# PSUM operands, a gate tile moved ahead of the attention, a shared score bank and chunks begun early, in a two-block fp32 transformer kernel

## The chip, the cores and the metric

The kernel runs on one core of a Trainium2 chip. The metric is the device time of one execution, in microseconds. The kernel before took 1399.2 us (median of 3 runs, 1398.55 to 1399.31).

## The reference

Two blocks work on one sequence of 512 tokens of width 1024, in fp32. The change touches the first block and the places where the blocks and their halves join:

```
mod = silu(c) @ ada_w + ada_b             # 6 rows of 1024: sh1 sc1 ga1 sh2 sc2 ga2
h = rmsnorm(x) * (1 + sc1) + sh1
glu, qkv, gates = split(h @ w_in)         # conv input, attention input, 2 x 1024 gate columns
u = silu(layernorm(causal_conv_31_taps(val * sigmoid(gate))))
z = q k^T / 8                             # stick-breaking attention, 8 heads of 64
a[t,s] = sigmoid(z[t,s]) * prod over s < j < t of sigmoid(-z[t,j])      # s < t
y = (sigmoid(g_conv) * (u @ w_conv_out) + sigmoid(g_att) * (a v @ w_att_out)) @ w_o
x = x + ga1 * rmsnorm(y)                  # boundary 1
x = x + ga2 * rmsnorm(swiglu(h2))         # h2 from rmsnorm(x), sc2, sh2; boundary 2
x = x + w_out(retention, latent attention); x = x + conv_ffn(rmsnorm(x))   # boundary 3 between
```

The second block and a last norm follow; their sources are unchanged.

## The kernel before, in words

Every fp32 product is three fp32r products (`mm3`, L202 to L205): high part by high part, low by high and high by low. A weight slab of 128x1024 is loaded by SP into `w_st`, ACT makes its high part `w_hi` (L185), and DVE or POOL the low part `w_lo` (L208). A weight tile is 8 x 3 = 24 products of 512 columns into one PSUM bank. There are 8 banks in three rings: `psT` with 2 (transposes, attention-by-value, modulation chunks), `psP` with 4 (function `pp()`: weight tiles and scores) and `psC` with 2 (convolution accumulators, later weight tiles too). The calls are written out in program order, and a scheduler orders each engine's instructions from a timing model of its own, so the queues below differ in places from the order of the source. Each engine then works its queue in order.

The stick-breaking stage (108 to 270 us): `stick_head` is a generator of three steps. In the first, for each of four query blocks `i` of 128, it takes a bank, writes (i+1)x128 score columns by three matmuls, and ACT writes sigmoid(-z) to `kp` and sigmoid(z) to `sp` (SBUF). DVE scans `kp` backwards into a running product (L739), and POOL (heads 0 to 5) or DVE multiplies `sp` by it (L743). The second step transposes the four blocks, the third multiplies by the values. `pipeline` runs the third step of head t-2, the second of t-1 and the first of t, and then `stick_between(t)`: weight tiles by the table `STICK_FILL` (q and k tiles of the next head pair, `g` gate tiles, `c` tiles of w_conv_out), some taps of the convolution, and modulation chunks by the table `AD`. The convolution's four channel blocks have 31 taps each: for blocks 0 to 2 one DVE operation a tap (L543, accumulator in PSUM), for block 3 a tap on ACT and an add on POOL (L547). Its sums `cacc` are then transposed on PE (L229) for the layer norm.

A modulation chunk (`ada_acc`) is 256 columns of `ada_w`, loaded as two halves `ad` of 512 KB. In mode "pe", 16 matmuls sum it over the rows (L376), in mode "dve" 8 DVE operations (L386, L388); then `ada_cols` or `ga_row` sums over the partitions by a matmul with `ones`, at once. In the merge (270 to 342 us), chunks run in mode "dve" behind each of four steps `p`. Steps 2 and 3 have two gate tiles and a w_conv_out slab each, every step has a w_att_out slab (24 products) and the gating on DVE and POOL.

At a boundary, `update` takes the two 512-column banks of a row tile: two squares on ACT give the norm, DVE multiplies by it and by the gate row into `y` (SBUF, L332), and `x + y` is done by DVE for the first half and by POOL for the second (L335). `boundary` then squares the 1024 new columns (`norm_of`) and scales them into `xn`, which PE transposes. Boundary 3 has no gate row: DVE adds straight from PSUM (L326).

Of the kernel before, what the change touches and what calls it, by code (L numbers as in the profile page):

```python
# [8 lines left out]
F32 = mybir.dt.float32  # L9
# [3 lines left out]
AF = mybir.ActivationFunctionType  # L13
# [6 lines left out]
KB = 8  # L20
# [76 lines left out]
def build(tc, nc, a):  # L97
# [145 lines left out]
    def sumsq(src, jp):  # L243
        ss = sm.tile([128, 1], F32, tag="ss", name="ss")
        n = src.shape[1]
        w = 256 if n <= 256 else 1024
        junk = jp.tile([128, w], BF16, tag=f"junk{w}", name="junk", bufs=1)
        nc.scalar.activation(out=junk[:, :n], in_=src, func=AF.Square, accum_out=ss)
        return ss
# [70 lines left out]
        return hh[:, k, :], hl[:, k, :]  # L320

    def update(banks, tt, x_in, x_out, grow, bp):
        if grow is None:
            for hf in range(2):
                cs = slice(512 * hf, 512 * hf + 512)
                nc.vector.tensor_tensor(out=x_out[:, cs], in0=banks[tt, hf], in1=x_in[:, cs], op=ALU.add)  # L326
            return
# [396 lines left out]
    def stick_head(h):  # L724
        p, b = divmod(h, 2)
        qs, ks, kl = qk[p]
        blocks = []
        for i in range(NT):
            n = (i + 1) * 128
            qb = slice(i * 128, n)  # L730
            z = pp()
            nc.tensor.matmul(out=z[:, :n], lhsT=qs[b][:, qb], rhs=ks[b][:, :n], start=True, stop=False)
            nc.tensor.matmul(out=z[:, :n], lhsT=qs[b][:, qb], rhs=kl[b][:, :n], start=False, stop=False)
            nc.tensor.matmul(out=z[:, qb], lhsT=identr, rhs=strict, start=False, stop=True)
            sp = apool.tile([128, n], F32, tag=f"sp{i}", name="sp")
# [3 lines left out]
            nc.vector.tensor_tensor_scan(  # L739
                out=kp[:, :n][:, ::-1], data0=kp[:, :n][:, ::-1], data1=zero.broadcast_to([128, n]),  # L740
                initial=1.0, op0=ALU.mult, op1=ALU.add,
            )
            (nc.gpsimd if h < 6 else nc.vector).tensor_tensor(  # L743
                out=sp[:, 0:n - 1], in0=sp[:, 0:n - 1], in1=kp[:, 1:n], op=ALU.mult
            )
            blocks.append(sp)
# [725 lines left out]
```

## Time and profile before

| | before |
|---|---|
| median of 3 runs | 1399.2 us (1398.55 to 1399.31) |
| profiled execution | 1396.24 us, span 1394.5 us |
| PE busy | 1351.0 us (97%), 6666 instructions |
| DVE, ACT, POOL busy | 777.8 (56%), 579.7 (42%), 333.1 us (24%) |
| DMA | 152.18 MB, mean 109 GB/s |
| mean granted TensorE clock | 0.992 |

The chain of work that ended last is 82% PE, 7% DVE, 4% ACT. Times are microseconds from the start of the profiled execution's span unless marked ns. A view by stretch gives each engine's busy time within a piece of the span, and PEclk the share of full speed that TensorE was granted there. In a row such as `ps_p<-hh,w_hi` the output stands left of the arrow; a bracket at the end is idle time just before the instruction and what ended it.

### The profile page before, as it was taken

The numbers are of one execution on the slowest core, as the hardware profiler recorded it, in microseconds if no ns is written. First come the engines' busy times: TensorE is split into PE (matmuls) and PEld (weight loads), VectorE is DVE, ScalarE is ACT, GpSimd is POOL, SyncE is SP. The second block draws the span as 40 slices with busy tenths as digits, with TensorE's granted clock in tenths as the row PEclk, the third lists the DMA queues.
The fourth block names the chain that finished last, engine by engine and source line by source line (L and its number), as shares of the span: only waits on it lengthen the run. The fifth ranks groups of instructions, "written<-read, shape, count | busy, mean of one in ns | idle before, by whom it ended". The sixth has DMA issues, their size and how long they took to land.

```text
span 1394.5 us, 17375 instructions
## 1 busy us (share of the span) xinstructions
PE 1351.0 (97%) x6666; PEld 1124.3 (81%) x6666; DVE 777.8 (56%) x1236; ACT 579.7 (42%) x953; POOL 333.1 (24%) x336
## 2 busy tenths in 40 slices
PE   8997999999989999999999999989999999999998
PEld 7786787888788888888887789777888888888886
DVE  5699878386357333323334655787257555554334
ACT  4557555332344222222224427777246433333323
POOL 2389665411150000000003434567020000000000
PEclk9998999999999999999999999999999999999999
DMA  9432133565125334433322332001323323323231
GB/s 339 143 97 67 58 119 107 184 225 183 64 68 174 121 112 130 126 101 91 104 92 82 128 102 87 24 25 46 121 76 122 105 91 100 97 93 104 91 99 68
DMA packets 44691, 152.18 MB, mean 109 GB/s; under 512 B 4913, under 2 KB 7473, under 8 KB 44609
## 3 DMA queue, kind: packets, MB, share of 16 engines
q1 hardware_dynamic: 43008, 146.03, 32.0%
q0 software_dynamic: 1312, 4.77, 1.0%
q8 instruction: 52, 0.85, 0.3%
q10 hardware_dynamic: 288, 0.27, 0.1%
q14 instruction: 31, 0.25, 0.1%
HBM read 146.86 MB, written 4.19 MB: 108 GB/s over the span
## 4 chain that ended last, share of the span: by engine, by line
PE 82%; DVE 7%; ACT 4%; issue 2%; POOL 2%; DMA 2%; SPq 0%; POOLq 0%; ACTq 0%; DVEq 0%
PE ps_p L203 16%; PE ps_p L204 16%; PE ps_p L205 16%; PE ps_c L203 7%; PE ps_c L204 7%; PE ps_c L205 7%; PE ps_t L203 2%; PE ps_t L204 2%; PE ps_t L205 2%; PE ps_t L229 2%; DVE w_lo L208 1%; DVE kp L739 1%; PE ps_t L699 1%; ACT w_hi L185 1%; DMA xs<-in_x 1%
## 5 line engine op out<-in xcount | busy, mean ns | idle before, releaser
L185 ACT CAST w_hi<-w_st 128x1024 fp32r<-128x1024 f32 (+2 forms) x217 | 225.3, 1040 | 386.6 <-PE ps_p L204 142.2
L208 DVE TENSOR_TENSOR w_lo<-w_st,w_hi 128x1024 fp32r<-128x1024 f32 (+2 forms) x179 | 221.6, 1240 | 239.8 <-ACT w_hi L185 238.4
L203 PE MATMUL ps_p<-hh,w_hi 128*128 128x512 f32 (+1 forms) x740 | 276.0, 380 | 4.2 <-ACT hh L264 3.2
L205 PE MATMUL ps_p<-hh,w_lo 128*128 128x512 f32 (+1 forms) x740 | 278.2, 377 | 1.4 <-DVE w_lo L208 1.4
L204 PE MATMUL ps_p<-hl,w_hi 128*128 128x512 f32 (+1 forms) x740 | 279.3, 379 | 0.2 <-POOL hl L208 0.2
L240 POOL TENSOR_TENSOR r<-q,mhalf 128x1 f32<-128x1 f32 x36 | 21.0, 584 | 768.5 <-DVE q L236 717.3
L203 PEld LDWEIGHTS ps_p<-hh,w_hi 128*128 128x128 f32 x740 | 139.4, 190 | 30.3 <-ACT hh L264 3.6
L205 PEld LDWEIGHTS ps_p<-hh,w_lo 128*128 128x128 f32 x740 | 140.8, 190 | 27.1 <-DVE w_lo L208 2.5
L204 PEld LDWEIGHTS ps_p<-hl,w_hi 128*128 128x128 f32 x740 | 140.9, 190 | 25.2 <-issue 0.8
L203 PE MATMUL ps_c<-hh,w_hi 128*128 128x512 f32 (+1 forms) x354 | 129.9, 367 | 3.2 <-ACT hh L264 2.0
L204 PE MATMUL ps_c<-hl,w_hi 128*128 128x512 f32 (+1 forms) x354 | 130.7, 370 | 0.6 <-POOL hl L208 0.6
L205 PE MATMUL ps_c<-hh,w_lo 128*128 128x512 f32 (+1 forms) x354 | 128.7, 364 | 0.0
L208 POOL TENSOR_TENSOR w_lo<-w_st,w_hi 128x1024 fp32r<-128x1024 f32 (+1 forms) x38 | 93.3, 2461 | 58.9 <-ACT w_hi L185 49.3
L208 DVE TENSOR_TENSOR gl<-gf,gh 128x512 fp32r<-128x512 f32 x44 | 30.4, 690 | 105.6 <-ACT gh L919 105.5
L919 ACT CAST gh<-gf 128x512 fp32r<-128x512 f32 x44 | 27.4, 622 | 133.4 <-PE ps_p L204 124.1
L203 PEld LDWEIGHTS ps_c<-hh,w_hi 128*128 128x128 f32 x354 | 67.3, 190 | 14.9 <-ACT hh L264 2.5
L204 PEld LDWEIGHTS ps_c<-hl,w_hi 128*128 128x128 f32 x354 | 67.2, 190 | 11.5 <-POOL hl L208 0.8
L205 PEld LDWEIGHTS ps_c<-hh,w_lo 128*128 128x128 f32 x354 | 67.3, 190 | 10.1
L205 PE MATMUL ps_p<-w_hi,gl 128*128 128x512 f32 x176 | 68.5, 389 | 0.0
L204 PE MATMUL ps_p<-w_lo,gh 128*128 128x512 f32 x176 | 68.5, 389 | 0.0
L203 PE MATMUL ps_p<-w_hi,gh 128*128 128x512 f32 x176 | 68.5, 389 | 0.0
L543 DVE SCALAR_TENSOR_TENSOR ps_c<-upad,vec,ps_c 128x512 f32<-128x512 f32 x87 | 60.6, 746 | 0.8
(430 smaller groups left out, 2579.0 us busy)
## 6 DMA issues: line engine op xcount, KB each, us to landing
ad<-in_ada SPq DMA_DIRECT2D x48, 512.0 KB, 4.1
w_st<-in_w_fin SPq DMA_DIRECT2D x44, 512.0 KB, 3.7
w_st<-in_w_up SPq DMA_DIRECT2D x44, 512.0 KB, 3.5
w_st<-in_w_win SPq DMA_DIRECT2D x22, 512.0 KB, 3.6
w_st<-in_w_fout SPq DMA_DIRECT2D x22, 512.0 KB, 3.6
w_st<-in_w_down SPq DMA_DIRECT2D x22, 512.0 KB, 3.5
w_st<-in_w_gate SPq DMA_DIRECT2D x16, 512.0 KB, 4.3
w_st<-in_w_wo SPq DMA_DIRECT2D x16, 512.0 KB, 3.7
```

Source lines behind the costliest of these rows:

```text
L185: nc.scalar.copy(w_hi[:, :n], w_st[:, :n])
L203: nc.tensor.matmul(out=out, lhsT=lh, rhs=rh, start=start, stop=False)
L204: nc.tensor.matmul(out=out, lhsT=lh, rhs=rl, start=False, stop=False)
L205: nc.tensor.matmul(out=out, lhsT=ll, rhs=rh, start=False, stop=stop)
L208: (eng or nc.vector).tensor_tensor(out=out, in0=src, in1=hi.bitcast(F32), op=ALU.subtract)
L229: nc.tensor.transpose(out=ps[:r, j * 128:(j + 1) * 128], in_=s, identity=ident)
L240: nc.gpsimd.tensor_tensor(out=r, in0=q, in1=mhalf[:, 0:1], op=ALU.pow)
L543: nc.vector.scalar_tensor_tensor(out=out, in0=src, scalar=w, in1=acc, op0=ALU.mult, op1=ALU.add)
L699: nc.tensor.matmul(out=ps[:, kb * 128:S], lhsT=vt(kb, h), rhs=a_slice(at[j], kb, 0, n), start=first, stop=kb == NT - 1 and j == 0,)
L739: nc.vector.tensor_tensor_scan(out=kp[:, :n][:, ::-1], data0=kp[:, :n][:, ::-1], data1=zero.broadcast_to([128, n]), initial=1.0, op0=ALU.m ...
L919: nc.scalar.copy(gh, gf[:, k, :])
```

## The change

Four things are rewritten.

In `stick_head`, blocks 0 and 2 (128 and 384 columns) share a bank, so a head takes three banks; `sp` is computed first, sigmoid(-z) is written over z in the bank, one ACT operation serves both blocks, and the scan reads the bank and writes `kp`. Gate tile 8 comes before head 0, and the tiles of `STICK_FILL` move up.

In `update`, `y` is written back into its bank, both adds are DVE's from PSUM, and each half is squared right after its add; `boundary` takes the norm from the two sums, at all three boundaries.

Chunk 5 of the second modulation goes from slot 8 of the stick stage (mode "pe") to step 0 of the merge (mode "dve"). `ada_cols` and `ga_row` begin a chunk and return the part with the `ones` matmul as a function, which the merge calls behind the step's products. The row chunks of `ga_row` are spread over steps 1 to 3, and three `ad` buffers are used in place of two.

```diff
-STICK_FILL = _fill("q1 k1|g8|q2 k2|g9|q3 k3|g10 g11|g12 g13|g14 g15|g0 g1 c0|g2 g3 c1")
+STICK_FILL = _fill("q1 k1|g9|q2 k2|g10|q3 k3|g11 g12|g13 g14|g15 g0|g1 c0|g2 g3 c1")
...
-ORDER += [("win", 8), ("win", 12)]
+ORDER += [("win", 8), ("win", 12), ("gate", 8)]
...
     def update(banks, tt, x_in, x_out, grow, bp):
-        if grow is None:
...
-        r = rstd(sumsq(banks[tt, 0], bp), sumsq(banks[tt, 1], bp), eps1k)
+        if grow is not None:
+            r = rstd(sumsq(banks[tt, 0], bp), sumsq(banks[tt, 1], bp), eps1k)
+        ss = []
         for hf in range(2):
             cs = slice(512 * hf, 512 * hf + 512)
-            y = bp.tile([128, 512], F32, tag="y", name="y", bufs=2)
...
-            (nc.vector if hf == 0 else nc.gpsimd).tensor_tensor(
-                out=x_out[:, cs], in0=x_in[:, cs], in1=y, op=ALU.add
-            )
+            y = banks[tt, hf]
+            if grow is not None:
+                nc.vector.scalar_tensor_tensor(out=y, in0=y, scalar=r, in1=grow[:, cs], op0=ALU.mult, op1=ALU.mult)
+            nc.vector.tensor_tensor(out=x_out[:, cs], in0=y, in1=x_in[:, cs], op=ALU.add)
+            ss.append(sumsq(x_out[:, cs], bp))
+        return ss
...
-            norm_of(xo, bp, xn)
+            nc.vector.tensor_scalar(out=xn, in0=xo, scalar1=rstd(ss[0], ss[1], eps1k), scalar2=None, op0=ALU.mult)
...
     def ada_cols(i, kb, g_name, ap_):
         acc, ps = ada_acc(8 * i + kb, ap_)
+        return lambda: ada_cols_end(i, kb, g_name, acc, ps)
...
-        for i in range(NT):
-            n = (i + 1) * 128
-            qb = slice(i * 128, n)
+        for grp in ((0, 2), (1,), (3,)):
             z = pp()
...
+            for i in grp:
+                n = (i + 1) * 128
+                qb = slice(i * 128, n)
+                zi = z[:, c0:c0 + n]
...
-            nc.scalar.activation(out=kp[:, :n], in_=z[:, :n], func=AF.Sigmoid, scale=-0.125)
-            nc.scalar.activation(out=sp, in_=z[:, :n], func=AF.Sigmoid, scale=0.125)
-            nc.vector.tensor_tensor_scan(
-                out=kp[:, :n][:, ::-1], data0=kp[:, :n][:, ::-1], data1=zero.broadcast_to([128, n]),
...
+            nc.scalar.activation(out=sp, in_=z[:, :c0], func=AF.Sigmoid, scale=0.125)
+            nc.scalar.activation(out=z[:, :c0], in_=z[:, :c0], func=AF.Sigmoid, scale=-0.125)
+            for i, cs in parts:
+                nc.vector.tensor_tensor_scan(
+                    out=kp[:, cs][:, ::-1], data0=z[:, cs][:, ::-1], data1=zero.broadcast_to([128, 128 * i + 128]),
...
-    AD = (3, 4, 5, 6, 7, 8, 20, 21)
+    AD = (3, 4, 5, 6, 7, 20, 20, 21)
...
+    att_gate(8)
     pipeline([stick_head(h) for h in range(NH)], (2, 1, 0), stick_between)
...
-    ADA.pool, ADA.tag, ADA.bufs, ADA.mode = mtmp, "ad", 2, "dve"
+    ADA.pool, ADA.tag, ADA.bufs, ADA.mode = mtmp, "ad", 3, "dve"
...
     for p in range(4):
+        accs = [accp, mtmp]
+        ends = [ada_cols(1, kb, "pre_ffn_g", accs.pop(0)) for kb in range(KB) if AD[kb] == 20 + p]
+        ends += [ga_row(0, grow1, accs.pop(0), q, mtmp) for q in ((), (0,), (1, 2), (3,))[p]]
...
-        for kb in range(KB):
-            if AD[kb] == 20 + p:
-                ada_cols(1, kb, "pre_ffn_g", accp)
-        for q in ((0,), (1, 2), (3,), ())[p]:
-            ga_row(0, grow1, accp, q, mtmp)
+        for end in ends:
+            end()
```

What moves is seen in the order of the queues. First SP's queue, ahead of the stick stage, before; `win` slabs are q and k tiles, the first two being q0 and k0:

```order
L184 DMA w_st<-in_w_v 128x1024 x2
L184 DMA w_st<-in_w_win 128x1024 x4
L184 DMA w_st<-in_w_gate 128x1024
L184 DMA w_st<-in_w_win 128x1024 x2
L184 DMA w_st<-in_w_gate 128x1024
L184 DMA w_st<-in_w_win 128x1024 x2
L361 DMA ad<-in_ada 128x1024 x2
```

The same place on SP now:

```order
L184 DMA w_st<-in_w_v 128x1024 x2
L184 DMA w_st<-in_w_win 128x1024 x2
L184 DMA w_st<-in_w_gate 128x1024
L184 DMA w_st<-in_w_win 128x1024 x2
L184 DMA w_st<-in_w_gate 128x1024
L184 DMA w_st<-in_w_win 128x1024 x2
L184 DMA w_st<-in_w_gate 128x1024
L184 DMA w_st<-in_w_win 128x1024 x2
L358 DMA ad<-in_ada 128x1024 x2
```

The slab of gate tile 8 is asked for ahead of q1 and k1, and each later gate slab one place sooner.

Second, DVE's queue around the first head, before; `kp<-kp,zero` is a scan (shown by the name of its form), `ps_c` and `cacc` are taps:

```order
L543 SCALAR_TENSOR_TENSOR cacc<-upad,vec,ps_c 128x512
L208 TENSOR_TENSOR kz_918<-ps_p,mv_997 64x512
L739 SCALAR_TENSOR_TENSOR kp<-kp,zero 128x128
L543 SCALAR_TENSOR_TENSOR cacc<-upad,vec,ps_c 128x512
L739 SCALAR_TENSOR_TENSOR kp<-kp,zero 128x256
L543 SCALAR_TENSOR_TENSOR ps_c<-upad,vec,ps_c 128x512
L739 SCALAR_TENSOR_TENSOR kp<-kp,zero 128x384
L543 SCALAR_TENSOR_TENSOR ps_c<-upad,vec,ps_c 128x512 x2
L739 SCALAR_TENSOR_TENSOR kp<-kp,zero 128x512
L543 SCALAR_TENSOR_TENSOR ps_c<-upad,vec,ps_c 128x512 x6
```

DVE's queue around the first head now:

```order
L546 SCALAR_TENSOR_TENSOR cacc<-upad,vec,ps_c 128x512
L208 TENSOR_TENSOR kz_918<-ps_p,mv_997 64x512
L546 SCALAR_TENSOR_TENSOR cacc<-upad,vec,ps_c 128x512
L546 SCALAR_TENSOR_TENSOR ps_c<-upad,vec,ps_c 128x512 x2
L748 SCALAR_TENSOR_TENSOR kp<-ps_p,zero 128x128
L748 SCALAR_TENSOR_TENSOR kp<-ps_p,zero 128x384
L748 SCALAR_TENSOR_TENSOR kp<-ps_p,zero 128x256
L546 SCALAR_TENSOR_TENSOR ps_c<-upad,vec,ps_c 128x512 x3
L748 SCALAR_TENSOR_TENSOR kp<-ps_p,zero 128x512
L546 SCALAR_TENSOR_TENSOR ps_c<-upad,vec,ps_c 128x512
```

The scans read `ps_p`, the score bank; three stand together, the 384 ahead of the 256, and more taps stand ahead of the first.

Third, PE's queue where the convolution's sums `cacc` are transposed for the first token tile, before (counted from q0 and k0, behind the scores of five heads and eight weight tiles):

```order
L203 MATMUL ps_p<-hh,w_hi 128x512
L204 MATMUL ps_p<-hl,w_hi 128x512
L205 MATMUL ps_p<-hh,w_lo 128x512
L229 MATMUL ps_p<-identr,cacc 128x128 x4
L376 MATMUL ps_t<-ad,cact 32x256 x8
L699 MATMUL ps_t<-al,v_656 128x512
```

PE's queue at the transposes of the third and fourth channel block of that token tile now (the first two stand behind head 0's scores), behind the scores of head 3:

```order
L738 MATMUL ps_p<-mv_1152,st_1102 128x512
L739 MATMUL ps_p<-kz_920,st_1102 128x512
L740 MATMUL ps_p<-mask,identr 128x128
L229 MATMUL ps_c<-identr,cacc 128x128
L702 MATMUL ps_t<-al,v_656 128x512
L702 MATMUL ps_t<-ah,v_656 128x512
...
L229 MATMUL ps_t<-identr,sp 128x128 x4
L229 MATMUL ps_c<-identr,cacc 128x128
L203 MATMUL ps_p<-hh,w_hi 128x512
```

The transposes go into a `psC` bank one by one, and the last two stand behind four heads' scores and six weight tiles: two tiles sooner.

## Rows read from the trace of the kernel before

**Rows 1.** page, busy time by engine: us (share of the span) x instructions

```profile
PE 1351.0 (97%) x6666; PEld 1124.3 (81%) x6666; DVE 777.8 (56%) x1236; ACT 579.7 (42%) x953; POOL 333.1 (24%) x336
```

**Rows 2.** windows: stretch, busy us by engine (x instructions), PEclk, DMA share, GB/s

```profile
108.20:113.90 5.70, 2.80 (x13) 2.02 (x13) 4.91 (x9) 5.58 (x12) 4.90 (x4) 0.87 0.52 137
113.90:125.80 11.90, 11.90 (x50) 9.76 (x49) 11.65 (x14) 7.55 (x13) 10.85 (x10) 0.92 0.06 25
...
126.50:132.40 5.90, 2.25 (x15) 1.70 (x13) 5.69 (x9) 5.59 (x12) 5.82 (x5) 1.00 0.28 89
...
125.80:134.50 8.70, 3.61 (x24) 2.95 (x22) 8.46 (x14) 7.66 (x15) 8.54 (x6) 0.91 0.33 102
134.50:147.20 12.70, 11.70 (x50) 9.46 (x48) 12.35 (x16) 7.59 (x16) 9.91 (x10) 0.79 0.03 13
270.00:342.00 72.00, 72.00 (x322) 59.66 (x321) 55.77 (x95) 21.52 (x27) 14.95 (x10) 1.00 0.59 191
380.00:417.00 37.00, 32.47 (x233) 29.27 (x232) 21.11 (x35) 18.67 (x36) 18.89 (x23) 0.95 0.20 65
742.00:792.00 50.00, 45.28 (x221) 36.54 (x221) 32.38 (x78) 27.16 (x68) 26.20 (x29) 1.00 0.29 102
985.00:1030.00 45.00, 43.41 (x225) 36.55 (x224) 19.71 (x31) 17.41 (x26) 8.85 (x8) 1.00 0.38 129
...
450.00:500.00 50.00, 50.00 (x222) 41.37 (x222) 20.18 (x27) 12.73 (x15) 0.00 (x0) 1.00 0.43 134
```

**Rows 3.** waits of PE, 108 to 160 us: total us, times, longest us

```profile
PE ps_p L732 <- ACT sp L738: 3.6, 2, 2.8
PE ps_p L732 <- ACT mv L665: 2.1, 1, 2.1
```

**Rows 4.** timeline of PE: start us, us, line, operation, output, inputs, shape

```profile
135.47 0.63 PE L205 MATMUL ps_p<-hh,w_lo 128*128 128x512 f32 x1
...
139.97 0.39 PE L204 MATMUL ps_p<-hl,w_hi 128*128 128x512 f32 x1
...
169.71 0.22 PE L732 MATMUL ps_p<-mv,st 128*128 128x128 f32 x1
169.86 1.07 PE L376 MATMUL ps_t<-ad,cact 128*32 128x256 f32 x16
```

**Rows 5.** timeline of DVE, three scans

```profile
115.19 1.65 DVE L739 TENSOR_TENSOR_SCAN kp<-kp,zero 128x256 f32<-128x256 f32 x1
...
141.31 1.53 DVE L739 TENSOR_TENSOR_SCAN kp<-kp,zero 128x512 f32<-128x512 f32 x1
...
163.96 0.69 DVE L739 TENSOR_TENSOR_SCAN kp<-kp,zero 128x256 f32<-128x256 f32 x1
```

**Rows 6.** timeline of ACT, the last sigmoid of head 1

```profile
138.37 0.59 ACT L738 ACTIVATE sp<-ps_p 128x512 f32<-128x512 f32 x1
```

**Rows 7.** timeline of POOL, the convolution's last add

```profile
155.00 2.21 POOL L547 TENSOR_TENSOR cacc<-cacc,tap 128x512 f32<-128x512 f32 x1
```

**Rows 8.** single lines: ns least/median/most, first and last start, shapes

```profile
L543 DVE SCALAR_TENSOR_TENSOR ps_c<-upad,vec,ps_c x87: 721/747/756, 67.2 to 152.4; 128x512 f32<-128x512 f32 x87
...
L547 POOL TENSOR_TENSOR cacc<-cacc,tap x30: 1258/1293/2213, 79.4 to 155.0; 128x512 f32<-128x512 f32 x30
...
L335 DVE TENSOR_TENSOR x<-x,y x8: 679/683/1623, 371.0 to 771.6; 128x512 f32<-128x512 f32 x8
...
L335 POOL TENSOR_TENSOR x<-x,y x8: 1282/1559/1668, 371.4 to 771.4; 128x512 f32<-128x512 f32 x8
...
L326 DVE TENSOR_TENSOR x<-ps_p,x x4: 681/687/691, 1013.8 to 1020.9; 128x512 f32<-128x512 f32 x4
...
L388 DVE SCALAR_TENSOR_TENSOR ps_t<-ad,cact,ps_t x36: 474/489/491, 272.4 to 323.7; 128x256 f32<-128x256 f32 x36
```

**Rows 9.** timeline of ACT, squares at boundary 1

```profile
379.65 1.06 ACT L248 ACTIVATE junk<-x 128x1024 bf16<-128x1024 f32 x1 [4.15 <-POOL x L335]
...
381.64 0.59 ACT L248 ACTIVATE junk<-ps_p 128x512 bf16<-128x512 f32 x1
```

More of the change, by code (lines that the diff above doesn't have):

```diff
@@ L322, in update @@
     def update(banks, tt, x_in, x_out, grow, bp):
-        if grow is None:
[L324 to L327, printed above, removed]
-        r = rstd(sumsq(banks[tt, 0], bp), sumsq(banks[tt, 1], bp), eps1k)
+        if grow is not None:
+            r = rstd(sumsq(banks[tt, 0], bp), sumsq(banks[tt, 1], bp), eps1k)
+        ss = []
         for hf in range(2):
             cs = slice(512 * hf, 512 * hf + 512)
-            y = bp.tile([128, 512], F32, tag="y", name="y", bufs=2)
-            nc.vector.scalar_tensor_tensor(
-                out=y, in0=banks[tt, hf], scalar=r, in1=grow[:, cs], op0=ALU.mult, op1=ALU.mult
-            )
-            (nc.vector if hf == 0 else nc.gpsimd).tensor_tensor(
-                out=x_out[:, cs], in0=x_in[:, cs], in1=y, op=ALU.add
-            )
+            y = banks[tt, hf]
[4 more added lines that the diff above has]
+        return ss
     def boundary(gen, x_in, x_out, grow, scale, bias, bp, after=None, ends=(1, 3)):
@@ L342, in boundary @@
             xi, xo = x_in(tt), x_out(tt)
-            update(banks, tt, xi, xo, grow, bp)
+            ss = update(banks, tt, xi, xo, grow, bp)
             xn = bp.tile([128, D], F32, tag="xn", name="xn", bufs=3)
-            norm_of(xo, bp, xn)
+            nc.vector.tensor_scalar(out=xn, in0=xo, scalar1=rstd(ss[0], ss[1], eps1k), scalar2=None, op0=ALU.mult)
             if after:
@@ L397, in ada_cols, with ada_cols_end @@
         acc, ps = ada_acc(8 * i + kb, ap_)
+        return lambda: ada_cols_end(i, kb, g_name, acc, ps)
+    def ada_cols_end(i, kb, g_name, acc, ps):
         for s in range(2):
@@ L418, in ga_row, with ga_row_end @@
         acc, ps = ada_acc(16 + 4 * i + q, ap_)
+        return lambda: ga_row_end(grow, cs, gr, acc, ps)
+    def ga_row_end(grow, cs, gr, acc, ps):
         nc.tensor.matmul(out=ps[:, 0:256], lhsT=ones, rhs=acc, start=True, stop=True)
@@ L480, in glu_mod @@
         ADA.mode = GLU_ADA[kb]
-        ada_cols(0, kb, "pre_mix_g", adp)
+        ada_cols(0, kb, "pre_mix_g", adp)()
         ADA.mode = "pe"
@@ L726, in stick_head @@
         qs, ks, kl = qk[p]
-        blocks = []
-        for i in range(NT):
-            n = (i + 1) * 128
-            qb = slice(i * 128, n)
+        blocks = [None] * NT
+        for grp in ((0, 2), (1,), (3,)):
             z = pp()
[L732 to L735, printed above, removed]
-            kp = apool.tile([128, S], F32, tag="kp", name="kp")
-            nc.scalar.activation(out=kp[:, :n], in_=z[:, :n], func=AF.Sigmoid, scale=-0.125)
-            nc.scalar.activation(out=sp, in_=z[:, :n], func=AF.Sigmoid, scale=0.125)
-            nc.vector.tensor_tensor_scan(
-                out=kp[:, :n][:, ::-1], data0=kp[:, :n][:, ::-1], data1=zero.broadcast_to([128, n]),
[L741 to L746, printed above, removed]
@@ new lines, in stick_head @@
+            parts, c0 = [], 0
+            for i in grp:
+                n = (i + 1) * 128
+                qb = slice(i * 128, n)
+                zi = z[:, c0:c0 + n]
+                nc.tensor.matmul(out=zi, lhsT=qs[b][:, qb], rhs=ks[b][:, :n], start=c0 == 0, stop=False)
+                nc.tensor.matmul(out=zi, lhsT=qs[b][:, qb], rhs=kl[b][:, :n], start=False, stop=False)
+                nc.tensor.matmul(out=zi[:, qb], lhsT=identr, rhs=strict, start=False, stop=i == grp[-1])
+                parts.append((i, slice(c0, c0 + n)))
+                c0 += n
@@ new lines, in stick_head @@
+            sp = apool.tile([128, c0], F32, tag=f"sp{grp[0]}", name="sp")
+            kp = apool.tile([128, S], F32, tag="kp", name="kp")
+            nc.scalar.activation(out=sp, in_=z[:, :c0], func=AF.Sigmoid, scale=0.125)
[3 more added lines that the diff above has]
+                    out=kp[:, cs][:, ::-1], data0=z[:, cs][:, ::-1], data1=zero.broadcast_to([128, 128 * i + 128]),
+                    initial=1.0, op0=ALU.mult, op1=ALU.add,
+                )
+                m = slice(cs.start, cs.stop - 1)
+                (nc.gpsimd if h < 6 else nc.vector).tensor_tensor(
+                    out=sp[:, m], in0=sp[:, m], in1=kp[:, cs.start + 1:cs.stop], op=ALU.mult
+                )
+                blocks[i] = sp[:, cs]
@@ L815, in stick_between @@
             if AD[kb] == t:
-                ada_cols(1, kb, "pre_ffn_g", accp)
+                ada_cols(1, kb, "pre_ffn_g", accp)()
         if t in (4, 6, 8):
             split_o(t // 2 - 2)
-    AD = (3, 4, 5, 6, 7, 8, 20, 21)
+    AD = (3, 4, 5, 6, 7, 20, 20, 21)
     ofs, oh, ol = {}, [], []
@@ L870, in build @@
             lo_of(ml_[:, m, :], gs[j], mh[:, m, :])
-        for kb in range(KB):
-            if AD[kb] == 20 + p:
-                ada_cols(1, kb, "pre_ffn_g", accp)
-        for q in ((0,), (1, 2), (3,), ())[p]:
-            ga_row(0, grow1, accp, q, mtmp)
+        for end in ends:
+            end()
     ADA.pool, ADA.tag, ADA.bufs = ring, "st", NST
@@ L977, in fin_extra @@
         if m in (4, 8, 12, 16):
-            ga_row(1, grow2, ad2, m // 4 - 1)
+            ga_row(1, grow2, ad2, m // 4 - 1)()
         if m == 4:
```

## The prediction

> **What bounds the kernel now.** I read the busy shares first: TensorE (PE) works 97% of the span, VectorE (DVE) 56% [rows 1], so a microsecond off another engine counts only where PE waits for it. PE's idle time is 43.5 us of 1394.5. The table by stretch shows where it lies [rows 2]: while the first heads of the stick-breaking attention run (108 to 147 us) PE is busy 2.80 of 5.70, 11.90 of 11.90, 3.61 of 8.70 and 11.70 of 12.70 us, so 9.0 us are lost; the three boundaries lose 4.5 (380 to 417), 4.7 (742 to 792) and 1.6 us (985 to 1030); a plain stretch of FFN loses nothing and shows 222 products in 50 us, 0.225 us each. The second loss is the clock, in the same rows: granted 0.87, 0.92, 0.91 and 0.79. [...] Busy time times the missing clock is 0.4 + 1.0 + 0.3 + 2.5 = 4.2 us. Then the waits of this stretch [rows 3]: scores for the key/query evacuations on ACT (2.1 us) and, twice, for a head's last sigmoid to free a score bank (3.6 us). Behind those sigmoids stand DVE and POOL, which fill these stretches nearly to the end (11.65 and 10.85 of 11.90 us, 8.46 and 8.54 of 8.70): convolution taps, scans and products of two or three heads stand in their queues.
>
> **Score banks, sigmoids, scan.** A head takes three banks in place of four and six sigmoids in place of eight. Before, heads 0 and 1 need eight allocations from a ring of four, so the last block of head 1 waits for a bank of head 0 (the 2.8 us of [rows 3]); with three, head 1's first group starts on a free one. Price on the other side: the keep probability is written into the bank and the scan reads it there, so a bank is held until DVE gets to its scan, not until ACT is through. For head 1's last block that is 142.84 against 138.96 us [rows 5, 6]: 3.9 us longer. In the forecast the product tiles between two heads (10.9 us for two of 24 products) cover that; see the second rival.
> A scan has two SBUF operands before, one afterwards. The 256-wide scan takes 0.69 us with POOL quiet and 1.65 beside a POOL add [rows 5], and POOL's adds, 1.29 us in the median, stretch to 2.21 in turn [rows 7, 8]. DVE's taps, with one operand in PSUM, show 721/747/756 ns (least, median, most) over 87 records [rows 8]: they are never stretched. So per head about 1.0 + 0.4 + 0.3 us of stretching goes; both ends, 0 and 2 us a head for the three heads beside the taps.
> [...]
> An add from PSUM takes 687 ns against 683 from SBUF, a tap, which also writes PSUM, 64 ns more than that [rows 8]: for 32 scans 0.1 to 2.0 us. I take the former, as the nearer operation, and call it 0.
>
> **Gate tile 8 ahead of head 0.** 24 products, 5.4 us, fill the gap at 108.2 in which PE waits 2.1 us for the mv evacuation [rows 3] and then waits again inside head 0's scores. They aren't new work: the tile is missing later, where each slot's tile moves up by one and slot 8 has one fewer. SP fetches its slab two slabs sooner; POOL and ACT split it earlier, which puts a 2.4 us POOL instruction ahead of head 0's products on POOL.
>
> **The sum of the stage.** Where does PE stand in before when it has done gates 8 and 9, q1, k1, q2, k2 and the scores of four heads? At 169.71 [rows 4]. Without idle time and at full clock the same content is 144 products x 0.225 = 32.4, four heads' scores at 2.1 (2.25 busy for one head and 3 transposes in 126.5 to 132.4, [rows 2]), 16 value products and 24 transposes (5.6, an estimate by their 128 to 512 columns from a 512-column product): 46.4 us, so 154.6. By idle and clock, 9.0 + 4.2 = 13.2 us is the most that can go. What is late next: in the new order PE meets the transposes of the convolution's third and fourth channel block just here, ahead of the next gate tile, and they wait for DVE and POOL. POOL's last add ends at 157.2 before [rows 7]; POOL idles 0.8 + 1.0 + 0.2 + 2.8 = 4.8 us up to 147.2 [rows 2], of which I give back about half: done at 154.5 to 155.5. PE will be there a little sooner and wait 2 to 3 us, which may cost clock again. So of 13.2 I take 10; bounds 4 (only the first gap and the stretching) and 13.
>
> **Chunks of the modulation.** Chunk 5 moves from slot 8, where PE sums it in 16 matmuls, 1.07 us together by an earlier chunk [rows 4], into the merge, where DVE does it in 8 operations of 489 ns [rows 8], 3.9 us. PE: -1.0. DVE in the merge goes from 55.77 to 59.7 of 72 us [rows 2] and a seventh chunk, 2 loads of 512 KB, joins SP's queue at a DMA share of 0.59. PE is busy 72.00 of 72 us there, so any wait is new: I take +0.5, bounds 0 and +4. Begun before a step's products and summed behind them, a chunk has those products as cover; steps 0 and 1 have just 24 products each (5.4 us) for two chunks each (7.8 us).
>
> **Boundaries.** Last row tile of boundary 1: y is done, POOL adds x 1.56 us (median, [rows 8]), ACT squares 1024 columns in 1.06 us [rows 9], then the root, then xn. Afterwards DVE adds in 0.69 and the square that counts is the second half, 0.59 us by the row of a 512 square [rows 9]: 0.9 + 0.5 = 1.4 us off the chain. New on DVE: an add of 0.69 per tile, while it is busy 21.11 of 37 us; a bank is held 0.7 us longer. PE loses 4.5 us in this stretch, some of it to later links, so I take -1.0 for boundary 1, -1.0 for boundary 2, and -0.5 for boundary 3, which has no POOL add to lose; together -2.5, bounds +1 and -5. The second block is otherwise reordered by the scheduler without a change of its work: 0, bounds ±2.5.
>
> **Sum.** -10 - 1.0 + 0.5 - 2.5 = -13.0 us on the profiled execution's 1396.24: 1383.2. That execution is 3.0 us under the median of the runs, 1399.2, so on their scale 1386.2.
>
> **Rivals.**
> 1. DVE and POOL stay the bound until the convolution is done. For it: both are over 90% busy in 113.9 to 134.5, and the change removes no tap. Against it: three heads' stretching goes. PE then merely arrives earlier at the conv transposes; the waits reappear there and only contention (about 5 us) and the other terms (-3) are kept: 1391.2.
> 2. Slower: held score banks. With keep probabilities in PSUM, a bank comes free only after its scan, which stands behind taps in DVE's queue. If products, which draw on the same four banks, need one while three are held, PE waits up to the 3.9 us of [rows 5, 6], at about 3 us a head. It decides from the fifth head on (15 us against 13 gained); six heads cost 18: 1386.2 + 18 = 1404. Against it: the taps end at about 157 us, after which scans come at once, so three or four heads can pay; and a tile between two heads needs one bank.
> 3. The merge pays. Ones-sums stand in PE's order behind each step; where a chunk's DVE chain of 3.9 us or its DMA is late, PE stops, in steps 0 and 1 above all (7.8 us of DVE work under 5.4 of products). +3 to +8 over the forecast, 1391.7 in the middle.
> 4. The change gives nothing where it is aimed, since the scheduler, which reorders all engines, spends it elsewhere (second block +2.5, late slot with a tile fewer +4, and so on): 1396 to 1400.
>
> **How the numbers follow.** Forecast 0.57, rivals 0.22, 0.06, 0.11 and 0.04. About 2.8 us (0.2%) is what a measurement of this kernel tells from no change. The first case is faster throughout, rival 1 nearly so (0.20 of 0.22), rival 3 mostly (0.09 of 0.11), rival 2 slower (0.04 of 0.06), rival 4 spread: faster 0.87, same 0.08, slower 0.05. The range goes from the stage's 13 with boundaries at -5 (1386.2 - 3.0 - 2.5 = 1380.7) to the upper end of rival 3 (1394.2), which takes in rival 1.
>
> **What would show it.** Right: PE busy without a gap from 60 to 115 us; no wait of scores on sp; the wait on mv gone; scans of 256 at about 0.7 us beside POOL; the fourth head's scores done before 157 us where 169.7 stood; a new wait of L229 ps_c on POOL cacc of 2 to 3 us; no POOL x in the boundaries, PE idle there 8 us in place of 11. Wrong: scores or gate products waiting on DVE kp (rival 2); the conv transposes waiting over 6 us (rival 1); PE under 71 of 72 us in the merge with ps_t waiting on DVE acc (rival 3); scans as long as before or longer.

## The result and the profile after

The changed kernel took 1384.9 us (median of 4 runs, 1383.2 to 1385.36) against 1398.88 for the kernel before: ratio 0.9905, 95% interval 0.9889 to 0.9921. The forecast was 1386.2, in a range of 1380.7 to 1394.2. The profiled execution took 1385.36 us, its span is 1383.2, 11.3 less than before. The page's first line answers to [rows 1]:

```profile
PE 1345.9 (97%) x6650; PEld 1124.4 (81%) x6650; DVE 768.5 (56%) x1251; ACT 581.5 (42%) x961; POOL 311.1 (22%) x328
```

The stretches of [rows 2] again, in the kernel after (the last three begin 12 to 13 us earlier, as the work does):

```profile
108.20:113.90 5.70, 5.70 (x31) 4.88 (x30) 4.80 (x8) 4.34 (x8) 4.94 (x3) 1.00 0.45 153
113.90:125.80 11.90, 11.90 (x57) 9.86 (x57) 9.81 (x14) 9.30 (x17) 11.71 (x10) 1.00 0.21 52
125.80:134.50 8.70, 5.21 (x26) 4.34 (x25) 8.56 (x14) 8.06 (x16) 7.71 (x8) 0.83 0.34 114
134.50:147.20 12.70, 12.70 (x67) 10.91 (x66) 12.36 (x19) 8.33 (x15) 10.99 (x10) 0.98 0.13 41
258.00:330.00 72.00, 72.00 (x325) 59.38 (x325) 57.51 (x105) 22.01 (x29) 15.72 (x10) 1.00 0.68 219
368.00:404.00 36.00, 32.59 (x236) 30.70 (x235) 21.45 (x36) 17.97 (x39) 15.02 (x21) 0.91 0.21 67
729.00:780.00 51.00, 47.88 (x229) 39.85 (x228) 32.92 (x83) 28.77 (x77) 20.10 (x25) 0.97 0.29 100
```

PE runs without a gap at full clock up to 125.8 us, where before it stood 2.9 us and ran at 0.87 and 0.92. One gap of 3.5 us is left; the clock is 0.83 in its stretch, 0.50 right behind the gap (131.7 to 134.5 us).

PE's waits from 108 to 160 us, which answer to [rows 3]:

```profile
PE ps_p L203 <- ACT ah L692: 3.5, 1, 3.5
PE ps_p L203 <- DVE kp L748: 0.7, 1, 0.7
```

Neither wait of before is there. The new 3.5 us is the first product of gate tile 9, behind head 1's scores; here PE, then DVE and ACT at that time:

```profile
127.84 0.39 PE L229 MATMUL ps_t<-identr,sp 128*128 128x128 f32 x2
131.71 0.76 PE L203 MATMUL ps_p<-hh,w_hi 128*128 128x512 f32 x1 [3.49 <-ACT ah L692]
```

```profile
130.64 0.92 DVE L748 TENSOR_TENSOR_SCAN kp<-ps_p,zero 128x384 f32<-128x384 f32 x1
...
131.49 0.66 DVE L748 TENSOR_TENSOR_SCAN kp<-ps_p,zero 128x256 f32<-128x256 f32 x1
```

```profile
131.04 0.98 ACT L692 CAST ah<-ps_t 128x512 fp32r<-128x512 f32 x2
132.04 0.58 ACT L667 CAST mv<-ps_p 64x512 fp32r<-64x512 f32 x1
```

The product doesn't read `ah`. It needs a `psP` bank: one is k1's, which ACT still reads at 132.04, three are head 1's, and the first of these comes free when the 384 scan of the shared bank ends, at 131.56, 0.15 us before the product. At the 0.7 us wait, where the view names DVE, it is the same: the 384 scan ends at 158.50, the product starts at 158.65.

```profile
157.57 0.93 DVE L748 TENSOR_TENSOR_SCAN kp<-ps_p,zero 128x384 f32<-128x384 f32 x1
```

That is the mechanism of the prediction's second rival, at one head.

Scans and POOL's adds by line (shapes of [rows 8], least/median/most ns):

```profile
L748 DVE TENSOR_TENSOR_SCAN kp<-ps_p,zero x27: 407/684/1224, 117.2 to 229.5; 128x256 f32<-128x256 f32 x8, 128x512 f32<-128x512 f32 x7, 128x128 f32<-128x128 f32 x6, 128x384 f32<-128x384 f32 x6
...
L748 DVE TENSOR_TENSOR_SCAN kp<-ps_c,zero x5: 415/932/1212, 188.9 to 224.2; 128x128 f32<-128x128 f32 x2, 128x384 f32<-128x384 f32 x2, 128x512 f32<-128x512 f32 x1
...
L550 POOL TENSOR_TENSOR cacc<-cacc,tap x30: 1263/1296/1325, 78.6 to 156.3; 128x512 f32<-128x512 f32 x30
```

No scan is longer than 1.22 us (3.01 before) and no add longer than 1.33 (2.21 before). The 32 scans, five of them from banks of `psC`, take 24.7 us in place of 38.4.

Since the profiled executions differ by up to 6 us before k0 ends (it ends between 105.5 and 111.7 us in the 14 profiles of this study), I take stretches from PE's timeline: k0's end (the start of the first score, less the 5.44 us of a gate tile or the 2.10 us of the wait ahead of it) to the first `w_hi,mh` product of the w_o gemm; on to the first `w_hi,gh` of the FFN's second half (boundary 1); to the first `identr,cT` of the second block (boundary 2); to the last `identr,rq`; to the end. The row for the second mark, after:

```profile
326.99 0.58 PE L203 MATMUL ps_t<-w_hi,mh 128*128 128x512 f32 x1
```

| us | k0 to w_o | to FFN out | to block 2 | to rq | to the end | sum |
|---|---|---|---|---|---|---|
| before | 229.85 | 299.16 | 160.75 | 85.72 | 503.77 | 1279.25 |
| after | 219.61 | 298.13 | 160.01 | 85.72 | 505.43 | 1268.90 |
| difference | -10.2 | -1.0 | -0.7 | 0.0 | +1.7 | -10.35 |

Each stretch is read from one profile. `phase` (below) differs from the change only in a line behind the first block and shows 220.3 there, so a difference of 0.7 us between two profiles says little.

### The profile page after: what moved, and what is told of

Same layout as the page of the kernel before. It is cut to its first block, busy times and chain, and to the rows that moved or that the text cites. A ratio compares the mean times of both kernels' runs of the same rounds, so it can differ in the third digit from the quotient of the medians.

```text
span 1383.2 us, 17379 instructions
## 1 busy us (share of the span) xinstructions
PE 1345.9 (97%) x6650; PEld 1124.4 (81%) x6650; DVE 768.5 (56%) x1251; ACT 581.5 (42%) x961; POOL 311.1 (22%) x328
## 4 chain that ended last, share of the span: by engine, by line
PE 88%; ACT 4%; DVE 4%; DMA 2%; issue 2%; POOL 0%; SPq 0%; POOLq 0%; ACTq 0%; DVEq 0%
PE ps_p L203 18%; PE ps_p L205 18%; PE ps_p L204 18%; PE ps_c L203 8%; PE ps_c L204 8%; PE ps_c L205 8%; PE ps_t L229 2%; PE ps_t L203 2%; PE ps_t L205 2%; PE ps_t L204 2%; PE ps_t L702 1%; ACT w_hi L185 1%; DMA xs<-in_x 1%; ACT sp L1261 1%; DVE w_lo L208 0%
## 5 line engine op out<-in xcount | busy, mean ns | idle before, releaser
L203 PE MATMUL ps_p<-hh,w_hi 128*128 128x512 f32 (+1 forms) x788 | 289.4, 374 | 8.6 <-ACT hh L264 3.9
L204 PE MATMUL ps_p<-hl,w_hi 128*128 128x512 f32 (+1 forms) x788 | 294.2, 374 | 0.0
L205 PE MATMUL ps_p<-hh,w_lo 128*128 128x512 f32 (+1 forms) x788 | 292.4, 372 | 1.2 <-DVE w_lo L208 1.1
L203 PEld LDWEIGHTS ps_p<-hh,w_hi 128*128 128x128 f32 x788 | 148.3, 190 | 34.7 <-ACT hh L264 4.4
L203 PE MATMUL ps_c<-hh,w_hi 128*128 128x512 f32 (+1 forms) x306 | 115.3, 377 | 0.3 <-ACT w_hi L185 0.3
L204 PE MATMUL ps_c<-hl,w_hi 128*128 128x512 f32 (+1 forms) x306 | 114.3, 373 | 0.0
L205 PE MATMUL ps_c<-hh,w_lo 128*128 128x512 f32 (+1 forms) x306 | 114.3, 373 | 0.0
L203 PEld LDWEIGHTS ps_c<-hh,w_hi 128*128 128x128 f32 x306 | 58.3, 190 | 10.7 <-ACT w_hi L185 0.6
L205 PEld LDWEIGHTS ps_c<-hh,w_lo 128*128 128x128 f32 x306 | 57.9, 189 | 9.8
L204 PEld LDWEIGHTS ps_c<-hl,w_hi 128*128 128x128 f32 x306 | 57.9, 189 | 9.6
```

The costliest lines, as they stand in the source:

```text
L203: nc.tensor.matmul(out=out, lhsT=lh, rhs=rh, start=start, stop=False)
L204: nc.tensor.matmul(out=out, lhsT=lh, rhs=rl, start=False, stop=False)
L205: nc.tensor.matmul(out=out, lhsT=ll, rhs=rh, start=False, stop=stop)
```

## Experiments

Letters: A is the score part (shared bank, scan from PSUM), B the gate tile, C the boundaries, D the modulation chunks. Ratios are to the kernel before as measured with each run (medians 1397.2 to 1399.0 us), with 95% intervals.

**Each part alone.** `gate_only` is B:

```diff
-STICK_FILL = _fill("q1 k1|g8|q2 k2|g9|q3 k3|g10 g11|g12 g13|g14 g15|g0 g1 c0|g2 g3 c1")
+STICK_FILL = _fill("q1 k1|g9|q2 k2|g10|q3 k3|g11 g12|g13 g14|g15 g0|g1 c0|g2 g3 c1")
...
+    att_gate(8)
```

> Only the gate tile is moved: tile 8 ahead of head 0, later tiles one slot earlier; the rest is the kernel before. Theory J (the stage's gain needs both the tile and the new score banks): the 2.1 and 0.75 us waits around head 0 go and the clock stays at 1.00 up to head 1, but scores still wait for the fourth bank and scans still stretch to 1.6 us: 3 to 5 us faster, about 1395. Rival G (the tile alone does it, since PE then stays one tile ahead of DVE and POOL throughout): 8 to 10 us faster, about 1390, and no wait of scores on sp longer than 1 us.

Measured: 1393.86 us, 0.9977 (0.9966 to 0.9987). k0 to w_o 227.66. The first waits go, one of 2.2 us for a score bank stays, and a new one stands in the merge (250 to 340 us), first PE's, then what DVE waits for there:

```profile
PE ps_t L419 <- DVE acc L388: 2.5, 3, 1.7
```

```profile
DVE ps_t L388 <- DMA ad<-in_ada: 4.3, 3, 2.8
DVE ps_t L386 <- DMA ad<-in_ada: 3.2, 2, 2.9
```

Theory J's size holds; rival G falls. PE reaches the merge sooner, the chunks don't: DVE waits 7.5 us for their loads here, 7.4 us in the same stretch of the kernel before.

`stick_only` is A:

```diff
-        for i in range(NT):
...
+        for grp in ((0, 2), (1,), (3,)):
...
-            nc.scalar.activation(out=kp[:, :n], in_=z[:, :n], func=AF.Sigmoid, scale=-0.125)
...
+            nc.scalar.activation(out=z[:, :c0], in_=z[:, :c0], func=AF.Sigmoid, scale=-0.125)
```

> Only the score part is changed: blocks 0 and 2 share a bank, the keep probability is written in PSUM and scanned from there; the gate tile stays in its slot. Theory J: the 2.1 us wait on mv stays, the waits of scores on sp (3.6 us) go, scans of 256 take 0.7 us: 4 to 7 us faster, about 1393. Rival G: within 2 us of the kernel before. Rival H (held banks): a product waits on a scan for 3 us at several heads, and the run is slower than before.

Measured: 1396.83 us, 0.9993 (0.9982 to 1.0003). k0 to w_o 227.85. Scores wait on no bank, but PE waits from 106 to 160 us elsewhere:

```profile
PE ps_t L229 <- DVE al L208: 4.0, 1, 4.0
PE ps_p L735 <- ACT mv L665: 2.1, 1, 2.1
```

The first of these is head 0's own: both `psT` banks hold its first seven transposes, and the last three stand 4.0 us until DVE has split the first four. Before, PE spent 3.6 us there on score banks and then waited 1.4 for the same split; so most of the wait moved rather than went. Rival G's "within 2 us" is what came; J was too high by 4 us.

`bound_only` is C:

```diff
-            (nc.vector if hf == 0 else nc.gpsimd).tensor_tensor(
-                out=x_out[:, cs], in0=x_in[:, cs], in1=y, op=ALU.add
...
+            nc.vector.tensor_tensor(out=x_out[:, cs], in0=y, in1=x_in[:, cs], op=ALU.add)
+            ss.append(sumsq(x_out[:, cs], bp))
```

> Only the update and the boundaries are changed. Theory J: PE's idle time at boundaries 1 to 3 (10.8 us together) falls by 2 to 2.5, and nothing else moves: 1396.5. Rival S (the scheduler reorders the second block by itself): the boundaries gain 2, the retention stage loses 2, 1398.5 to 1399.

Measured: 1394.42 us, 0.9978 (0.9969 to 0.9987). By stretch -1.1 (boundary 1), -1.2 (boundary 2), -0.4 behind rq: -2.6, as theory J said.

`merge_only` is D:

```diff
-    AD = (3, 4, 5, 6, 7, 8, 20, 21)
+    AD = (3, 4, 5, 6, 7, 20, 20, 21)
...
+        for end in ends:
+            end()
```

> Only the modulation chunks are changed: chunk 5 to the merge, chunks begun ahead of a step's products and summed behind them, three buffers. Theory J: PE loses the 1.0 us of 16 matmuls, the merge's 72 us grow by 0.5 at most: 1398.4. Rival M (the merge pays): PE idle over 2 us between 270 and 342 us, ps_t waiting on acc: 1400 to 1402.

Measured: 1396.53 us, 0.9988 (0.9978 to 0.9997). k0 to w_o 229.85, no different: the 16 matmuls are gone, but PE is busy only 0.4 us less there (219.8 against 220.2) and idle 0.4 us more; its granted clock from 108.2 to 160 us was 0.87 against 0.90. What is measured lies behind rq (-1.0), where D changes no work.

**Pairs and threes.** The four parts alone give -10.2 us in k0 to w_o only in company: B -2.2, A -2.0, D 0.0, sum -4.2. `stick_gate` is A and B, `gate_merge` B and D, `no_gate` A, C and D; their edits are those above.

> Gate tile and score banks together, boundaries and chunks as before. Alone, the two shortened the stretch from the end of k0 to the first w_o product from 229.9 us to 227.7 and 227.9; the whole change made it 219.6. Theory P (the pair interacts: PE runs ahead only if neither the empty queue nor the banks stop it): 221 to 223 us, 1390 us. Rival M (the chunks are what lets the gain through, since with the gate tile alone PE waited 2.5 us on acc in the merge): 225 us or more, 1393, with ps_t waiting on acc for over 2.5 us.

Measured: 1392.64 us, 0.9958 (0.9946 to 0.9970); k0 to w_o 223.73, and PE waits 1.9 us on acc in the merge. Between the two theories: P's stretch was 221 to 223, M's 225 and more.

> Gate tile and chunks, scores and boundaries as before. Theory P: the wait of 2.2 us for a score bank and the stretched scans stay, so 225 to 227 us from k0 to w_o, 1393 us. Rival M: the 2.5 us on acc go and most of the gain is there: 221 to 223 us, 1390 us.

Measured: 1390.28 us, 0.9946 (0.9929 to 0.9963); k0 to w_o 223.67, no wait on acc. Between the two again.

> The whole change without the gate tile's move. Theory P: the 2.1 us wait on mv and waits of about 4 us on al behind head 0 return, 226 to 228 us from k0 to w_o, boundaries give 2.5: 1393 us. Rival G (the tile's place is of no weight once banks are shared): 1387 or less.

Measured: 1393.94 us, 0.9975 (0.9965 to 0.9985); k0 to w_o 226.32. Theory P: the waits on mv (2.1 us) and on al (4.1 us) are back.

The stretch adds up as B -2.2; D on top of B -4.0 (227.66 to 223.67); A on top of both -4.1 (to 219.61); or in another order A on top of B -3.9, D on top of both -4.1. So D gives 4 only where the gate tile has moved, and A 4 there too. On D without the gate tile A gives 3.5 (229.85 to 226.32, `no_gate`; C, which that run has too, leaves this stretch at 229.94). D is four things at once, the chunk moved, chunks begun early, a third buffer and row chunks a step later; no run took them apart.

**What of A carries it.** `sbuf_scan` is the whole change, but the keep probability and the scan are in SBUF:

```diff
-            nc.scalar.activation(out=z[:, :c0], in_=z[:, :c0], func=AF.Sigmoid, scale=-0.125)
+            nc.scalar.activation(out=kp[:, :c0], in_=z[:, :c0], func=AF.Sigmoid, scale=-0.125)
...
-                    out=kp[:, cs][:, ::-1], data0=z[:, cs][:, ::-1], data1=zero.broadcast_to([128, 128 * i + 128]),
+                    out=kp[:, cs][:, ::-1], data0=kp[:, cs][:, ::-1], data1=zero.broadcast_to([128, 128 * i + 128]),
```

> The whole change, but the keep probability goes to SBUF and the scan reads and writes it there, so it has two SBUF operands again; the shared bank and six sigmoids stay, and a bank is free when ACT is through. Theory H (PE's 3.5 us wait at 131.7 us is for head 1's first bank, held until its scans): the wait falls under 1.5 us; scans beside POOL stretch to 1.6 us again and POOL's adds to 2.2; the two nearly cancel: 1384 to 1387. Rival C (contention is what mattered): the convolution ends 4 us or more later, 1389 or more. Rival A (that wait is for ACT's queue, not for the bank): it stays over 3 us.

Measured: 1400.61 us, 1.0024 (1.0012 to 1.0036): slower than the kernel before. k0 to w_o 233.68, 14 us more than with the scan in PSUM. First the scans' line, with what DVE waited for ahead of them; then that of POOL's products, with who waited for them:

```profile
L748 DVE TENSOR_TENSOR_SCAN kp<-kp,zero x32: 406/925/2937, 119.8 to 243.8; 128x128 f32<-128x128 f32 x8, 128x384 f32<-128x384 f32 x8, 128x256 f32<-128x256 f32 x8, 128x512 f32<-128x512 f32 x8
...
  ACT kp L746: 8.1, 6
```

```profile
L753 POOL TENSOR_TENSOR sp<-sp,kp x24: 630/1021/1376, 120.5 to 204.5; 128x127 f32<-128x127 f32 x6, 128x383 f32<-128x383 f32 x6, 128x255 f32<-128x255 f32 x6, 128x511 f32<-128x511 f32 x6
...
  ACT kp L746: 8.4, 7
```

The scans take 34.8 us (24.7 from PSUM), POOL's adds stretch to 2.20 again, and DVE's last tap ends 53.2 us behind k0's end in place of 45.4. Besides that there is a ring: ACT can't write a keep probability before POOL has read an older one out of one of the two `kp` buffers (8.4 us), and DVE waits for ACT (8.1 us). With the keep probability in PSUM ACT doesn't write `kp` at all. The two causes weren't separated. The 3.5 us wait behind head 1 is gone, as theory H says, but the price is far above it; rival C was right.

`psum_four` is the whole change without the sharing:

```diff
-        for grp in ((0, 2), (1,), (3,)):
+        for grp in ((0,), (1,), (2,), (3,)):
```

> The whole change without the sharing: each score block has a bank of its own again (four a head, eight sigmoids), the keep probability is still written in PSUM and scanned there. With the scan moved to SBUF and the bank shared the stretch from k0 to w_o took 233.7 us against 219.6. Theory O (the operand carries it, the sharing little): 219 to 222 us, 1384 to 1387, scans of 256 at 0.7 us. Rival B (fewer banks carry it): scores wait 3 us and more for banks held until their scans, 226 us or more, 1391 or more.

Measured: 1391.13 us, 0.9952 (0.9939 to 0.9966); k0 to w_o 225.17, 1.5 more than with the old scores (223.67). Scans are short, but PE waits from 100 to 340 us:

```profile
PE ps_t L229 <- DVE al L208: 4.4, 3, 3.5
PE ps_p L203 <- DVE kp L748: 1.6, 1, 1.6
```

So here scanning from PSUM pays only with a bank fewer per head, and the bank fewer only with the scan in PSUM: -4.1 together, +1.5 and +10.0 by halves (the ring is part of the latter). Rival B's time was nearer, but no score waits 3 us for a bank, as it had it: transposes wait.

**What is left.** `phase` sets the bank counter back ahead of the second block, `fill_even` deals the tiles out evenly, `small_first` is `phase` with the group of one block first:

```diff
+    Banks.at = (Banks.at + 2) % 6
```

```diff
-STICK_FILL = _fill("q1 k1|g9|q2 k2|g10|q3 k3|g11 g12|g13 g14|g15 g0|g1 c0|g2 g3 c1")
+STICK_FILL = _fill("q1 k1|g9 g10|q2 k2|g11 g12|q3 k3|g13 g14|g15 g0|g1|g2 c0|g3 c1")
```

```diff
-        for grp in ((0, 2), (1,), (3,)):
+        for grp in ((1,), (0, 2), (3,)):
```

> The whole change and one line more, which sets the counter that hands out psP and psC banks two steps on ahead of the second block, since heads now call for 8 banks fewer; the second block then has its former banks and nearly its former order. Theory K (the shifted banks cost the retention and latent attention 1.6 to 2 us): the time from the last rq transposes to the end falls from 505.4 to 503.8 us, 1383. Rival N (it is the profiled runs' spread): no change, 1385.

Measured: 1385.83 us, 0.9918 (0.9904 to 0.9931). The stretch behind rq is 503.78 us, as theory K has it, 1.65 less than after; the whole time doesn't show so little, its interval overlaps that of the change. Whether it is the banks, see the end of the next section. PE's waits on sp from 880 to 960 us, first in the kernel after, then with the counter set back:

```profile
PE ps_p L203 <- ACT sp L1261: 2.1, 2, 1.8
PE ps_c L203 <- ACT sp L1261: 2.0, 2, 1.3
```

```profile
PE ps_c L203 <- ACT sp L1262: 1.9, 2, 1.0
...
PE ps_p L203 <- ACT sp L1262: 1.7, 3, 0.9
```

> The whole change with the fill tiles dealt two to each of the first seven slots: q1 k1, g9 g10, q2 k2, g11 g12, q3 k3, g13 g14, g15 g0, then g1, g2 c0, g3 c1. Theory W (PE's 3.5 us wait and the 0.7 us one stand behind the slots with a single tile, while DVE and POOL still work on taps): the product that meets a held bank is the first of the slot whatever its length, but the wait falls due once per head, so PE gains only what DVE and POOL can follow: 2 us faster at most, 1383 to 1385. Rival L (later slots with a single tile open a new gap behind head 7): 1386 to 1389.

Measured: 1388.63 us, 0.9940 (0.9923 to 0.9957); k0 to w_o 222.42. The 3.5 us wait is unchanged, and a new one of 2.0 us on kp stands at 225 us, between the scores of heads 6 and 7. The time is rival L's, its place, behind head 7, isn't.

> The whole change, the second block's banks set back as in phase, and the groups in the order (1), (0, 2), (3), so that a head's first bank holds one block and is free after one scan of 0.7 us, where it took three scans of 1.8 us together. Theory H (PE's 3.5 us wait behind head 1 is for its first bank): the wait is 2.5 us or less, 218.5 us or less from k0 to w_o, and with 503.8 us behind the last rq transposes 1382 to 1384. Rival A (the wait has nothing to do with the bank): it stays at 3.3 us or more. Rival O (order: the shared bank, with two scans behind one sigmoid pair, comes free later and the wait only moves to the next tile): 1386 or more.

Measured: 1384.06 us, 0.9890 (0.9873 to 0.9906). PE's waits from 106 to 340 us:

```profile
PE ps_t L229 <- DVE al L208: 4.1, 2, 2.3
PE ps_p L203 <- ACT gat L810: 0.2, 1, 0.2
```

But for 0.2 us no product waits for a bank any more, which speaks for theory H; but 4.1 us of waits for transposes come in their place, and k0 to w_o is 220.3, not 218.5. That is what `phase` has too (220.3), from which this run differs by the order alone; by all stretches it is 0.7 us shorter than `phase` and 1.7 shorter than the change (1267.2, 1268.0 and 1268.9). The runs can't tell it from the change.

## Why the prediction was right

**The bound** was read right: PE is gapless at full clock up to 125.8 us, no score waits on mv or on a sigmoid for a bank, and the stretched scans and adds are gone, 13.7 us of scan time in all. One reading was wrong: head 1's last block did not wait 2.8 us for a bank of head 0. Three banks were head 1's own, k1's was still read by ACT at 133.40, and PE went on when head 1's first sigmoid was through. Before:

```profile
131.33 0.30 ACT L738 ACTIVATE sp<-ps_p 128x128 f32<-128x128 f32 x1
...
131.68 0.49 PE L732 MATMUL ps_p<-mv,st 128*128 128x512 f32 x1 [2.83 <-ACT sp L738]
```

The remedy holds all the same, since three banks a head fit beside k1's; what then meets the full ring is the next product tile.

**The sum of k0 to w_o** was right, its terms weren't. Forecast were -10 for scores and gate tile, -1.0 for the chunk on PE and +0.5 for the merge, -10.5; measured -10.2. But `stick_gate` gives -6.1 for the first and D on top of it -4.1 for the other two. Two steps failed. "So of 13.2 I take 10" counted PE's place when four heads' scores are done; that place was nearly right (these scores, head 1's value products and the last transpose of the first token tile end at 158.0, 50.6 us behind k0's end, against 61.4 before) and `stick_gate` gives back some 4.5 us behind it. "+0.5 ... bounds 0 and +4" saw in the chunks only a cost of the merge. In before PE came late enough for the chunks; once it comes 4 us and more sooner it waits 1.9 to 2.5 us for them, and with D that wait is gone (which part of D does it wasn't tested). The third rival had the right mechanism with the wrong sign: it is the old order that pays.

**The step "PE will be there a little sooner and wait 2 to 3 us"** named the wrong wait. The transposes of the convolution's sums came at 155.7 and 157.7, when DVE (152.8) and POOL (157.6) were through, POOL only just:

```profile
157.05 0.62 PE L229 MATMUL ps_t<-identr,sp 128*128 128x128 f32 x4
157.65 0.33 PE L229 MATMUL ps_c<-identr,cacc 128*128 128x128 f32 x1
158.65 0.47 PE L203 MATMUL ps_p<-hh,w_hi 128*128 128x512 f32 x1 [0.67 <-DVE kp L748]
```

```profile
153.50 4.10 POOL L550 TENSOR_TENSOR cacc<-cacc,tap 128x512 f32<-128x512 f32 x3
```

The weight load of the last transpose waits 0.2 us for POOL. The forecast had POOL done at 154.5 to 155.5, half its idle time given back; it was done no sooner, 50.2 us behind k0's end against 48.9 before, though none of its adds is stretched any more. Had PE not stood 3.5 us earlier on, it might have waited here for POOL after all; no run shows it.

PE stood 3.5 us for a held bank instead, and 0.7 us at 158.65. The second rival priced this at 3 us a head; it fell due at one head, and 0.7 us at another. That the stage's sum came out with this wait in the forecast one's place is luck. Why the other heads go free (more tiles in the slots, the end of the taps) is argued, not shown. That the bank is what this wait is for rests on the times above, on `sbuf_scan`, where it is gone, and on `small_first`, where a bank is free sooner; no run changed the bank alone.

**The boundaries** were forecast at -2.5. By stretch C gives -1.0 and -0.7 after and -2.6 in all by itself; PE's waits at boundary 1 go from 5.0 us (372 to 422 us, before) to 4.2 (360 to 410, after), and none is behind POOL any more. The first rows before, then after:

```profile
PE ps_c L203 <- ACT hh L264: 2.0, 2, 1.5
PE ps_c L203 <- ACT w_hi L185: 0.8, 1, 0.8
PE ps_c L204 <- POOL hl L208: 0.6, 1, 0.6
```

```profile
PE ps_t L229 <- DVE hf L269: 2.3, 1, 2.3
PE ps_p L203 <- ACT hh L264: 0.8, 1, 0.8
```

**The operand in PSUM** cost nothing at these shapes: an add from PSUM takes 683 ns in the median, as from SBUF [rows 8], the 256 scan 0.66 us against 0.69 from SBUF with POOL quiet.

```profile
L332 DVE TENSOR_TENSOR x<-ps_p,x x12: 680/683/692, 366.1 to 1007.1; 128x512 f32<-128x512 f32 x12
```

**The second block**, 0 with bounds of ±2.5, came at +1.7, and its cause stays open. 8 calls for a bank fewer come before it, so its banks are handed out in another turn, and `phase`, which undoes that, has the waits of before again and 1.65 us less. But the waits make no difference: PE is idle 10.3 us behind rq after and 10.2 in `phase`; 1.5 us lie in its busy time, at a lower granted clock:

```profile
870.85:1376.28 505.43, 495.12 (x2444) 414.74 (x2443) 282.73 (x427) 221.90 (x373) 74.75 (x94) 0.99 0.27 86
...
872.98:1376.76 503.78, 493.59 (x2443) 413.65 (x2442) 278.03 (x427) 221.26 (x373) 74.80 (x94) 1.00 0.27 86
```

And `fill_even`, with the turn of the change, has 503.5. The six profiles with that turn lie between 503.5 and 505.4, the eight with the turn of before between 502.4 and 504.2.

By spans the change gives 11.3 us, by medians 14; the profiled execution of before was 3 us faster than its median, and the start up to k0's end differs by more than that from run to run. By stretches it gives 10.4 where 13.0 was forecast, mostly for the second block, which with boundary 3 was put at -0.5 and came at +1.7. That the forecast time lies within 1.3 us of the median is so in part luck: against the medians of before in the later rounds (1397.2 to 1399.0) the change gives 12.3 to 14.1.

## What to carry to other kernels

Parts of a change that each look worth 2 us can be worth 10 together and 4 by themselves: when PE is made to arrive sooner, the next thing it meets decides, and that must be moved too. Here POOL's longest add was 1.33 us with the scan's data in PSUM and 2.20 with them in SBUF (`sbuf_scan`), but head 1's first bank was held 2.6 us longer than ACT needed it (ACT through at 128.95 us, the scan at 131.56); free a bank in the same change. Compare stretches between marks on the timeline where whole times of a few us spread more than the effect.

## What the runs showed of the hardware

A scan with data in SBUF, whose second operand is only a broadcast zero column in SBUF, was slowed beside POOL (a 256 one 1.65 us, 0.69 with POOL quiet [rows 5]) and slowed POOL in turn: the 32 scans took 38.4 us (before) and 34.8 (`sbuf_scan`) with their data in SBUF, and 24.7 with it in PSUM; POOL's longest add was 2.21, 2.20 and 1.33 us. Why the place of the data matters is not shown, nor whether the zero column has a part in it.

In the kernel after, the granted clock was 1.00 through 17.6 us of gapless work (108.2 to 125.8 us) and 0.83 in the stretch with the one gap of 3.5 us: 0.50 from the gap's end at 131.7 to 134.5 us, where a 512-column product shows 0.63 us in place of 0.39.
